# Cosine-similarity attention on one core: six shared PSUM banks for scores and transposes, and exponentials of three, two and three banks

## The chip, the core and the metric

The kernel runs on one core of one Trainium2 chip. The core has five engines that run side by side and meet only at semaphores: TensorE (PE in the profile, its weight loads PEld), VectorE (DVE), ScalarE (ACT), GpSimd (POOL) and SyncE (SP), which here only issues transfers. Inputs and output lie in HBM, the working data in SBUF, and what TensorE computes lands in PSUM, which has eight banks of 512 fp32 columns for each of 128 partitions. The metric is device time in microseconds (us), the median over runs. Before the change it is 190.81 us (three runs, 190.81 to 190.95).

## What is computed

Q, K and V are fp32 of shape (8, 12, 512, 64): 96 heads of 512 rows and 64 columns. Each row of Q and K is divided by its length, the scores of a head are the dot products divided by tau = 0.1, and softmax weights of them are applied to V:

```
Q_norm = Q / (np.linalg.norm(Q, axis=-1, keepdims=True) + 1e-10)
K_norm = K / (np.linalg.norm(K, axis=-1, keepdims=True) + 1e-10)
scores = np.einsum('bhqd,bhkd->bhqk', Q_norm, K_norm) / tau
weights = np.exp(scores - np.max(scores, axis=-1, keepdims=True))
weights = weights / (np.sum(weights, axis=-1, keepdims=True) + 1e-10)
return np.einsum('bhqk,bhkd->bhqd', weights, V).astype(np.float32)
```

A score lies between -10 and 10, so the kernel leaves the maximum out and takes exp(score / tau) as it is. The sum of the weights comes out of the product with V, through a column of ones beside V.

## The kernel before

The 96 heads are worked on as 48 pairs (index s, from 0 to 47). The work on a pair is a chain of small operations, each with a name:

- LD and LV: transfers of Q, K (into the tile qk) and V (vf), issued by SP.
- SQ: squares of Q and K, on POOL (on ACT for a part of the first three pairs).
- RED: the row sums of the squares, on DVE, one for Q (w = 0) and one for K (w = 1). For K, and for both in the first pairs, PE first adds eight slices into a corner of an output bank (SSQ), and DVE reduces what is left.
- NEW: one over the square root of the sums, for a group of 1, 2 or 4 pairs. Groups 1 to 3 (one pair each) do it on ACT (LOG, then NEW), the others in eight or nine short dependent steps on DVE.
- SCL: Q and K times that root, giving bf16 (qn). Q is scaled on DVE, K on POOL or, for ten pairs, on DVE.
- TR: eight transposes on PE into PSUM; EVA: one DVE copy of them into SBUF (qt).
- SCO: scores. A key chunk c (128 keys) of head h is one matmul with 64 rows of the array and 512 columns, so it fills one PSUM bank. Head 0 uses array rows 0 to 63 and head 1 rows 64 to 127.
- EXP: ACT reads score banks and writes exp of them in bf16 (et).
- PV: for each head four groups (t) of four small matmuls, et as weights and V with the column of ones as data, into an output bank (o_ps[h]).
- RCP and NRM: DVE takes the reciprocal of the sums and multiplies; ST: the transfer out. VC on POOL turns V into bf16.

The eight PSUM banks are dealt out so: four for scores (scps), two for outputs (ops), one for transposes (tps), one for the norm work (nps). The four score banks are used in two halves. One EXP takes 1024 columns, that is, chunk c of both heads; while ACT works on one half PE refills the other. So a pair is four SCOs of two matmuls and four EXPs. In pair 0 the first two chunks are taken head by head (four EXPs of 512 columns), and the last chunk of pair 47 is cut in three pieces (256, 512, 256 columns) so that the last products can start early.

The order of the work is written out by hand, one list of operation numbers for each engine (ORDER, L574). Each engine runs its list in order and waits for the operations that its next one needs (Program.run, L41). The lines that matter below: the scores are issued at L446 and the exponentials at L469 (the last pieces at L460), PV at L486 (L514 for the last pair), the transposes at L410 (L256 and L254 in pair 0), EVA at L417 (L267 in pair 0), SCL at L404, SSQ at L342, RED at L349 and L353, the root on ACT at L367 and L370 and on DVE at L377 to L386, NRM at L499 and L527, and the last stores at L531.

Of the kernel before, what the change touches and what calls it, by code (L numbers as in the profile page):

```python
# [8 lines left out]
class Op:  # L9
    def __init__(self, key, eng, kind, due, needs, emit, slot=None):  # L10
        self.key, self.eng, self.kind, self.due, self.emit = key, eng, kind, due, emit
        self.needs, self.slot = [n for n in needs if n is not None], slot
        self.own = False
        self.sem, self.val, self.inc, self.used = None, 0, 0, False
        self.start = self.end = None


class Program:


    def __init__(self, nc):
        self.nc, self.ops, self.list = nc, {}, []

    def add(self, key, eng, kind, due, needs, emit, **kw):
        assert key not in self.ops, key
        op = Op(key, eng, kind, due, needs, emit, **kw)
        self.ops[key] = op
        self.list.append(op)
        return op

    def schedule(self):
        order = {}
        for e, text in ORDER.items():
            order[e] = [self.list[int(x)] if x[0] != "-" else self.dummy(int(x[1:])) for x in text.split()]
        assert len(self.list) == len({o.key for v in order.values() for o in v if o.key != "dummy"})
        return order

    def dummy(self, columns):
        return Op("dummy", "pe", "", 0, [], lambda e: self.fill(e, columns))

    def run(self):  # L41
        nc = self.nc
        order = self.schedule()
        dma_sems, dma_count, last_out = {}, {}, {}
        for e, ops in order.items():
            for o in ops:
                o.waits = [self.ops[n] for n in o.needs]
                if e in ("pe", "act") and not o.own:
                    o.waits = [p for p in o.waits if p.eng != e]
                for p in o.waits:  # L50
                    p.used = True
        for e, ops in order.items():
            sem, count = nc.alloc_semaphore(f"s_{e}"), 0
            for o in ops:
# [8 lines left out]
                elif o.used:  # L63
                    count += 1
                    o.sem, o.val, o.inc = sem, count, 1

        def write(engine, name):
            seen = {}
            for o in order[name]:
                want = {}  # L70
                for p in o.waits:
                    k = id(p.sem)
                    if p.val > max(seen.get(k, 0), want.get(k, (None, 0))[1]):
                        want[k] = (p.sem, p.val)
                for k, (sem, val) in want.items():
                    engine.wait_ge(sem, val)
                    seen[k] = val
                inst = o.emit(engine)
                if o.sem is not None:
                    inst.then_inc(o.sem, o.inc)  # L80
# [26 lines left out]
def bass_cosine_similarity_attention_kernel(  # L107
# [11 lines left out]
    NP = BATCH * NHEAD // 2  # L119
    MAGIC = float(0x5F375A86)  # L120
# [13 lines left out]
    et = [sb(f"et{i}", [128, NT, 2, SEQ], bf16) for i in range(R_ET)]  # L134
    ob = [sb(f"ob{i}", [128, 2, NT, DIM], f32) for i in range(R_O)]
    rd = [sb(f"rd{i}", [128, 2, NT], f32) for i in range(R_O)]
    ys = [sb(f"ys{i}", [128, 64], f32) for i in range(R_X)]
    xs = {g: sb(f"xs{g}", [128, 64], f32) for g in NORM_ON_ACT}
# [6 lines left out]
    sc_ps = nc.alloc_psum_tensor("scps", [128, 4, SEQ], f32)  # L145
    o_ps = [nc.alloc_psum_tensor(f"ops{b}", [128, 512], f32) for b in range(2)]
    t_ps = nc.alloc_psum_tensor("tps", [128, 2, NT, 128], bf16)
    t_k0 = sc_ps[:, 3, :].bitcast(bf16)[:, 0:SEQ].rearrange("p (t x) -> p t x", t=NT)
    n_ps = nc.alloc_psum_tensor("nps", [128, R_X, 160], f32)
# [3 lines left out]
    sizes, left = [], NP  # L153
    for n in GROUPS:
        sizes.append(min(n, left))
        left -= sizes[-1]
        if not left:
            break
    while left:
        sizes.append(min(GROUPS[-1], left))  # L160
        left -= sizes[-1]
    group, first = [], []
    for g, n in enumerate(sizes):
        first.append(len(group))
        group += [g] * n
# [8 lines left out]
    P.add("one", "pool", "one", -100, [], lambda e: e.memset(ones[:, :], 1.0))  # L174
    P.add("eye", "pool", "sm_pool", -99, ["one"], lambda e: e.affine_select(  # L175
        out=ident[:, :], in_=ones[:, :], pattern=[[1, 128]], base=0, channel_multiplier=-1,
        compare_op=ALU.is_equal, fill=0.0))
    P.add("eps", "pool", "sm_pool", -98.5, [], lambda e: e.memset(eps[:, :], 1e-19))
    P.add("table", "act", "table", -900, [], lambda e: e.preload_act_table_set("natural_log_exp_and_others"))
    P.add("vone", "pool", "vone", -98, [], lambda e: e.memset(  # L180
# [7 lines left out]
    P.fill = lambda e, n: e.matmul(out=sc_ps[:, 0, 0:n], lhsT=ident[:, :], rhs=warm_in[:, 0:n], start=True, stop=True)  # L188
    P.add("wz", "dve", "sm_dve", -100, [], lambda e: e.memset(warm_in[:, :], 0.0))
    P.add("warm", "pe", "warm", -100, ["eye", "wz"], warm)  # L190

    def due_sq(s):
        g = group[s]
        return START + PERIOD * first[g] - 7.6 + (1.9 if g in NORM_ON_ACT else 0) - 3.43 * (first[g] + sizes[g] - 1 - s) - slack(s, M_SQ)

    def due_red(s):
        return due_sq(s) + 2.0

    slots = sorted((START + PERIOD * (s + 1) + 0.9 * PV_AT[4 * h + 3] + 0.05 + late(s), s, h) for s in range(NP - 1) for h in range(2))
    session, attached, early = {}, {}, []  # L200
    for s, w in sorted(((s, w) for s in range(NP) for w in range(2) if on_pe(s, w)), key=lambda j: (due_red(j[0]), j)):
        at = due_red(s) + 0.3
        if s < EARLY:
            early.append((s, w))
            continue
        due, i, h = next(x for x in slots if x[0] >= at and (x[1], x[2]) not in attached)
        attached[i, h] = (s, w)
        session[s, w] = (h, due, [("PV", i, h, NT - 1)])
    before = [[], []]
    for s, w in sorted(early):  # L210
        session[s, w] = (w, due_red(s), before[w])
        before[w] = [("RED", s, w)]
    bank_free = {}
    for s in range(NP):
        for h in range(2):
            bank_free[s, h] = before[h]
            before[h] = [("NRM", s, h)] + ([("RED",) + attached[s, h]] if (s, h) in attached else [])

    def head0(TF):
        for h in range(2):  # L220
            at = -100 + h
            x4 = [xs[0][:, 8 * w + 4 * h : 8 * w + 4 * h + 4] for w in range(2)]
            for w in range(2):
# [6 lines left out]
                P.add(("SQ", 0, w, h), SQ0[w][h], {"act": "sqah", "dve": "sqvh", "pool": "sqph"}[SQ0[w][h]], at + 0.1 * w,  # L230
                      [("LD", 0, w, h)] + (["table"] if SQ0[w][h] == "act" else []), emit)
                P.add(("RED", 0, w, h), "dve", "redh", at + 0.2 + 0.1 * w, [("SQ", 0, w, h)],
                      lambda e, w=w, x4=x4, dst=dst: e.tensor_reduce(out=x4[w], in_=dst, axis=AX.X, op=ALU.add))
            cols = lambda t, h=h: t[:, 0:16].rearrange("p (w x) -> p w x", w=2)[:, :, 4 * h : 4 * h + 4]
            P.add(("LOG", 0, h), "act", "ln", at + 0.4, [("RED", 0, 0, h), ("RED", 0, 1, h), "eps", "table"],
                  lambda e, cols=cols: e.activation(out=cols(ys[0]), in_=cols(xs[0]), func=ACT.Ln, bias=eps[:, :]))
            r_ps = sc_ps[:, 1, 0:4] if h == 0 else n_ps[:, 0, 128:132]
            for w in range(2):
                P.add(("NRMS", 0, w, h), "act", "sm_act", at + 0.5 + 0.01 * w, [("LOG", 0, h)],
                      lambda e, w=w, h=h, r_ps=r_ps: e.activation(  # L240
                          out=xs[0][:, 8 + 4 * h : 12 + 4 * h] if w else r_ps,
                          in_=ys[0][:, 8 * w + 4 * h : 8 * w + 4 * h + 4], func=ACT.Exp, scale=-0.5)).own = True
# [304 lines left out]
EARLY = 4  # L547
PE_BOTH = 4
K_ON_DVE = (1, 2, 3, 4, 9, 15, 21, 27, 33, 39)
VLAG = 3  # L550
# [143 lines left out]
```

## Time and profile before

| what | value |
|---|---|
| median of three runs | 190.81 us |
| span of the profiled execution, first to last instruction | 188.7 us |
| what lies around the span (the median less the span) | 2.1 us |
| ACT busy | 182.1 us (96%) |
| PE busy, ends modelled | 176.0 us (93%) |
| DVE busy | 164.9 us (87%) |
| POOL busy | 155.0 us (82%), all of it before about 165 us |
| DMA engines | 269 GB/s in the mean, most of it in the first 160 us |
| granted TensorE clock | full in all 40 slices of the span |

A row of the groups gives the source line, engine, operation, output and inputs with their shapes, how many instructions there are, how long the engine was busy with them in all, the mean length of one in ns, and what the engine waited for just before. The length of one instruction is longer than the distance to the next one: instructions of one engine overlap, and the distance is what counts for the sum. The chain of waits follows the work that ended last back to the start. In the timeline each line is a run of like instructions with its start, its length from first start to last end, and its count.

### The profile page before, as it was taken

The page shows a single profiled execution, that of the slowest core. Times are in us where ns is not written, and L with a number is a line of the kernel's source. Part 1 is how long each engine was busy: PE and PEld are TensorE (multiplying, and loading weights), DVE is VectorE, ACT ScalarE, POOL GpSimd, SP SyncE. Part 2 cuts the span into 40 slices and gives each one's busy share as a digit, 9 for nine tenths or more (in the row PEclk, how much of TensorE's full clock was granted, in tenths as well). Part 3 has the DMA queues.
Part 4 walks back from the last instruction along what each step waited for, and adds up shares of the span by engine and source line. Part 5 has one row for each costly group of instructions (what it writes and reads, how often), then busy time and mean ns, then how long its engine had stood idle before and what let it go on. Part 6 is the DMA issues. An engine that isn't in the chain of part 4 may idle for free.

```text
span 188.7 us, 6679 instructions
## 1 busy us (share of the span) xinstructions
PE 176.0 (93%) x2726; PEld 110.1 (58%) x2726; DVE 164.9 (87%) x530; ACT 182.1 (96%) x214; POOL 155.0 (82%) x145
## 2 busy tenths in 40 slices
PE   6998999999999999999999999999999999899992
PEld 2555666566665666566666566665666556555552
DVE  2789999999999899999999989998889987977543
ACT  4899999999999999999999999999999999999992
POOL 5689999999999999999999899999699898260000
PEclk9999999999999999999999999999999999999999
DMA  4999999999999978999898997997999943113133
GB/s 153 345 352 351 349 357 322 311 315 377 381 385 354 296 264 261 349 335 299 270 255 256 378 344 233 300 314 223 280 326 336 326 139 113 59 56 115 56 114 111
DMA packets 52445, 50.75 MB, mean 269 GB/s; under 512 B 3136, under 2 KB 52416, under 8 KB 52416
## 3 DMA queue, kind: packets, MB, share of 16 engines
q1 hardware_dynamic: 51984, 50.02, 81.6%
q8 instruction: 21, 0.34, 0.7%
q10 hardware_dynamic: 432, 0.33, 0.5%
q14 instruction: 8, 0.07, 0.1%
HBM read 37.75 MB, written 12.58 MB: 267 GB/s over the span
## 4 chain that ended last, share of the span: by engine, by line
ACT 94%; DMA 3%; SPq 1%; issue 1%; DVE 1%; PE 0%
ACT et L469 92%; DMA qk<-in_Q_dram 3%; SPq L299 0%; SPq L296 0%; ACT et L460 0%; DVE ob L527 0%; ACT sq L317 0%; ACT ys L367 0%; ACT nps L370 0%; PE ops L514 0%; DVE rd L525 0%
## 5 line engine op out<-in xcount | busy, mean ns | idle before, releaser
L469 ACT ACTIVATE et<-scps 128x1024 bf16<-128x1024 f32 (+1 forms) x193 | 175.8, 1247 | 0.0
L325 POOL TENSOR_TENSOR sq<-qk 128x1024 bf16<-128x1024 f32 x44 | 82.7, 1891 | 2.0 <-DMA qk<-in_K_dram 2.0
L446 PE MATMUL scps<-qt 64*128 64x512 bf16 x384 | 75.5, 385 | 7.4 <-ACT et L469 2.3
L486 PE MATMUL ops<-vb,et 128*128 128x65 bf16 x1504 | 74.5, 194 | 0.0
L486 PEld LDWEIGHTS ops<-vb,et 128*128 128x128 bf16 x1504 | 56.1, 98 | 27.9 <-issue 21.5
L404 POOL TENSOR_TENSOR qn<-qk,rk 128x512 bf16<-128x512 f32 x37 | 38.1, 1041 | 6.4 <-DVE rk L382 6.1
L499 DVE TENSOR_TENSOR ob<-ops,rd 128x256 f32<-128x256 f32 x94 | 39.3, 420 | 0.9
L404 DVE TENSOR_TENSOR qn<-qk,nps 128x512 bf16<-128x512 f32 x57 | 38.1, 678 | 0.4 <-ACT nps L370 0.4
L417 DVE COPY qt<-tps 128x1024 bf16<-128x1024 bf16 x47 | 32.3, 688 | 4.1 <-PE tps L410 3.4
L446 PEld LDWEIGHTS scps<-qt 64*128 64x128 bf16 x384 | 19.4, 92 | 26.1 <-ACT et L469 10.1
L410 PE MATMUL tps<-ident,qn 128*128 128x128 bf16 x376 | 33.0, 221 | 0.1
L474 POOL TENSOR_SCALAR vb<-vf 128x512 bf16<-128x512 f32 x48 | 29.3, 624 | 0.7 <-PE tps L410 0.7
L353 DVE TENSOR_REDUCE nps<-sq 128x8 f32<-128x512 bf16 x44 | 29.7, 683 | 0.0
L410 PEld LDWEIGHTS tps<-ident,qn 128*128 128x128 bf16 x376 | 21.4, 98 | 12.0 <-issue 5.7
L497 DVE RECIPROCAL rd<-ops 128x4 f32<-128x4 f32 x94 | 16.6, 177 | 9.2 <-PE ops L486 5.8
L342 PE MATMUL ops<-sq,ident 128*128 128x64 bf16 x400 | 20.0, 193 | 0.0
L342 PEld LDWEIGHTS ops<-sq,ident 128*128 128x128 bf16 x400 | 14.9, 98 | 4.1 <-issue 2.9
L349 DVE TENSOR_REDUCE nps<-ops 128x8 f32<-128x64 f32 x44 | 9.3, 211 | 0.8 <-PE ops L342 0.7
L377 DVE TENSOR_TENSOR nps<-nps,ys 128x32 f32<-128x32 f32 (+1 forms) x30 | 6.3, 208 | 0.2
L378 DVE SCALAR_TENSOR_TENSOR nps<-nps,ys 128x32 f32<-128x32 f32 (+1 forms) x30 | 6.2, 207 | 0.2
L185 PE MATMUL ops<-warm_in,ident 128*128 128x512 bf16 x8 | 3.6, 631 | 1.4 <-POOL ident L175 1.4
L319 POOL TENSOR_TENSOR sq<-qk 128x512 bf16<-128x512 f32 (+1 forms) x4 | 3.7, 933 | 1.2 <-DMA qk<-in_K_dram 1.0
(50 smaller groups left out, 40.8 us busy)
## 6 DMA issues: line engine op xcount, KB each, us to landing
vf<-in_V_dram SPq DMA_DIRECT2D x48, 256.0 KB, 5.3
qk<-in_Q_dram SPq DMA_DIRECT2D x47, 256.0 KB, 4.3
qk<-in_K_dram SPq DMA_DIRECT2D x47, 256.0 KB, 5.4
out_dram<-ob SPq DMA_DIRECT2D x47, 256.0 KB, 3.5
qk<-in_Q_dram SPq DMA_DIRECT2D x2, 128.0 KB, 2.7
qk<-in_K_dram ACTq DMA_DIRECT2D x2, 128.0 KB, 2.9
out_dram<-ob SPq DMA_DIRECT2D x1, 128.0 KB, 1.7
out_dram<-ob ACTq DMA_DIRECT2D x1, 64.0 KB, 1.6
```

The costliest lines, as they stand in the source:

```text
L325: lambda e: e.tensor_tensor(out=sqf, in0=data, in1=data, op=ALU.mult))
L342: last = e.matmul(out=o_ps[bank][:, 320:384], lhsT=ident[:, :], rhs=sq[iqs][:, 8 * w : 8 * w + 8, 8 * k : 8 * k + 8], start=(k == 0), stop ...
L353: lambda e, w=w, dst=dst: e.tensor_reduce(out=dst, in_=sq[iqs][:, 8 * w : 8 * w + 8, :], axis=AX.X, op=ALU.add))
L404: lambda e, w=w, r=r: e.tensor_tensor(out=qn[iqn][:, w].rearrange("p t h d -> p h t d"), in0=qk[iq][:, w].rearrange("p h (t d) -> p h t d" ...
L410: last = e.transpose(t_ps[:, w, t, :], qn[iqn][:, w, t].rearrange("p h d -> p (h d)"), ident[:, :])
L417: lambda e: e.tensor_copy(out=qt[iqt][:, :, :, :].rearrange("p w t x -> p (w t x)"), in_=t_ps[:, :, :, :].rearrange("p w t x -> p (w t x)")))
L446: last = e.matmul(out=sc_ps[:, 2 * b + h, :], lhsT=qt[iqt][64 * h : 64 * h + 64, 1, c, :], rhs=qt[iqt][64 * h : 64 * h + 64, 0, :, :], sta ...
L469: lambda e, c=c, b=b, hs=hs: e.activation(out=et[iet][:, c, hs[0] : hs[-1] + 1, :], in_=sc_ps[:, 2 * b + hs[0] : 2 * b + hs[-1] + 1, :], f ...
L474: lambda e: e.tensor_scalar(out=vb[:, iq, :, :, 0:DIM].rearrange("p c h d -> p h c d"), in0=vf[iv][:, :, :].rearrange("p h (c d) -> p h c ...
L486: last = e.matmul(out=o_ps[h][:, 65 * t : 65 * t + 65], lhsT=et[iet][:, c, h, 128 * t : 128 * t + 128], rhs=vb[:, iq, c, h, :], start=(c = ...
L497: lambda e, h=h, grid=grid: e.reciprocal(out=rd[io][:, h, :], in_=grid[:, :, DIM]))
L499: lambda e, h=h, grid=grid: e.tensor_tensor(out=ob[io][:, h], in0=grid[:, :, 0:DIM], in1=rd[io][:, h, :].unsqueeze(2).to_broadcast([128, N ...
```

## The change

- PSUM is dealt out anew: six banks form one ring that scores and transposes share, and two banks take outputs (numbers 6 and 7, o_ps[0] and o_ps[1]). The transpose bank and the norm bank are gone.
- From pair 9 on (WIDE = 9) the eight score banks of a pair go to ACT as three EXPs of 3, 2 and 3 banks in place of four of 2. The ring is used in halves of three: pair s takes banks 0-2, 3-4, 0-2 or 3-5, 0-1, 3-5 by turns. The third bank of the half that has only two banks of scores takes the transposes of the next pair. Pairs 1 to 8 keep four EXPs of two banks (banks 0-1 and 3-4), with transposes in bank 2.
- In pair 0 and pair 47 the scores go head by head (by_head): pair 0 in EXPs of 1, 1, 2, 2, 2 banks, pair 47 in 3, 2, and then 1280 and 256 columns. The spare bank for the last piece of the last product is the first bank of the middle half of the ring, where it was the transpose bank.
- Norm work: the sums (xs) and the running product (ys) lie in SBUF. The running root and the result lie in output bank 6, in columns 384 and up, and for groups 2 to 6 in ring bank 5. The DVE scaling reads its factor from there. All SSQ go to a corner of bank 7. In groups where K of some pair is scaled on DVE the result for Q and K is one step in place of two.
- Orders: one sequence over all engines in place of five lists. From it the program takes each engine's order, and it adds a wait between any two operations of different engines that touch the same bank, in the order of the sequence (link). Waits that earlier waits imply are left out. The ring of scaled tiles (qn) has four buffers in place of three. The orders of all engines are new; in pair 0 the LOG of group 1 stands after the second EXP and its NEW after the third, where they stood after the first.

The core of the diff:

```diff
-RINGS = 18, 10, 6, 3, 3, 3, 8, 3
+RINGS = 18, 10, 6, 4, 3, 3, 8, 3
+FIRST, FIRST_BANKS = (1, 1, 2, 2, 2), (0, 1, 3, 0, 3)
+WIDE = 9
+TURN0 = (2, 5)
+ROOT_BANK = {2: 5, 3: 5, 4: 5, 5:5, 6:5}
...
-    sc_ps = nc.alloc_psum_tensor("scps", [128, 4, SEQ], f32)
+    ring = nc.alloc_psum_tensor("ring", [128, 6, SEQ], f32)
     o_ps = [nc.alloc_psum_tensor(f"ops{b}", [128, 512], f32) for b in range(2)]
-    t_ps = nc.alloc_psum_tensor("tps", [128, 2, NT, 128], bf16)
-    n_ps = nc.alloc_psum_tensor("nps", [128, R_X, 160], f32)
+    O = (6, 7)
...
+    def by_head(s):
+        return s in (0, LAST)
+
+    def unit(s, c, h):
+        return NT * h + c if by_head(s) else 2 * c + h
+
+    plan, turn_bank, uses = [], {}, []
+    for s in range(NP):
+        lo, hi = (0, 3) if s < WIDE or (s - WIDE) % 2 == 0 else (3, 0)
+        turn_bank[s] = lo + 2
+        if s < WIDE:
+            counts = FIRST if s == 0 else (2, 2, 2, 2)
+            banks = FIRST_BANKS if s == 0 else (0, 3, 0, 3)
+        else:
+            counts, banks = (3, 2, 3), (lo, hi, lo)
...
+    def link(self, sequence):
+        touched = {}
+        for n, o in enumerate(sequence):
+            o.place = n
+            o.waits = [self.ops[k] for k in o.needs]
+            for b in o.banks:
+                last = touched.setdefault(b, {})
+                o.waits += [p for e, p in last.items() if e != o.eng and p not in o.waits]
+                last[o.eng] = o
...
+            def sco(e, units=units, b=b):
+                for k, (c, h) in enumerate(units):
+                    last = e.matmul(
+                        out=ring[:, b + k, :], lhsT=qt[iqt][64 * h : 64 * h + 64, 1, c, :],
+                        rhs=qt[iqt][64 * h : 64 * h + 64, 0, :, :], start=True, stop=True)
+                return last
...
+            for k, (lo, hi) in enumerate(((0, 1280), (1280, 1536)) if (s, j) == (LAST, 2) else ((0, n * SEQ),)):
+                P.add(("EXP", s, j + k), "act", f"exp{hi - lo}", [("SCO", s, j), "table"] + values,
...
+        xg, tg = xs[g % R_X][:, 0 : 2 * m], ys[g % R_X][:, 0 : 2 * m]
+        yg = bank[:, ROOTS : ROOTS + 2 * m]
+        rg = bank[:, col : col + 2 * m]
...
-                        t_ps[:, w, t, :], qn[iqn][:, w, t].rearrange("p h d -> p (h d)"), ident[:, :])
+                        turned(turn_bank[s])[:, w, t, :], qn[iqn][:, w, t].rearrange("p h d -> p (h d)"), ident[:, :])
```

Three stretches of the new sequence, its numbers turned into the names above (key chunk and head left out where they do not matter; w after a dash):

```
pair 1's start    ACT: SQ-2 EXP-0-0 EXP-0-1 LOG-1 EXP-0-2 NEW-1 EXP-0-3 EXP-0-4 LOG-2 NEW-2 EXP-1-0
                  PE:  SCO-0-0 SCO-0-1 SCO-0-2 SSQ-1-1 TR-0 SSQ-2-0 SCO-0-3 SSQ-2-1 SCO-0-4 TR-1-1
                       PV-0(1) SSQ-3-0 TR-1-0 PV-0(5) SSQ-3-1 SCO-1-0
                  DVE: RED-2-0 SCL-1-1 SCL-1-0 RED-2-1 RED-3-0 EVA-1 SCL-2-0
pair 22           EXP-22-0 | SCO-22-1 TR-23-1 TR-23-0 PV-21(4) EXP-22-1 | SCO-22-2 SSQ-29-1 EXP-22-2
pair 47's end     PE:  ... EXP-47-2 then PV-47 of both heads, the last after EXP-47-3
                  DVE: RCP-47-0 RCP-47-1 RCP-47-2 NRM-47-1 NRM-47-2 NRM-47-0
                  SP:  ST-47-0 ST-47-2
```

## The prediction

> **What bounds the kernel now.** I read the page's busy shares and chain first, then the chain in order of time, then ACT's groups by shape, then the timeline of PE, ACT and DVE at the start and in the middle.
>
> ```profile
> PE 176.0 (93%) x2726; PEld 110.1 (58%) x2726; DVE 164.9 (87%) x530; ACT 182.1 (96%) x214; POOL 155.0 (82%) x145
> ACT 94%; DMA 3%; SPq 1%; issue 1%; DVE 1%; PE 0%
> ...
> 14.79 169.56 ACT et L469 x185
> 184.34 0.78 ACT et L460 x2
> ```
>
> The chain is one row of exponentials: 185 of them in 169.56 us, 0.9165 us each, with nothing between. The kernel is ACT's time plus a start of some 8 us and an end of 3.3 us (last EXP's end, 185.39, to 188.73).
>
> ```profile
> L469 ACT ACTIVATE et<-scps 128x1024 bf16<-128x1024 f32 x189 | 173.6, 1261 | 0.0
> L469 ACT ACTIVATE et<-scps 128x512 bf16<-128x512 f32 x4 | 2.1, 586 | 0.0
> L317 ACT ACTIVATE sq<-qk 128x512 bf16<-128x512 f32 x2 | 1.3, 630 | 0.4 <-DMA qk<-in_Q_dram 0.3
> L317 ACT ACTIVATE sq<-qk 128x256 bf16<-128x256 f32 x1 | 0.4, 417 | 0.1
> ```
>
> From 256 to 512 columns a square grows by 213 ns, 0.832 ns a column. So 1024 columns are 852 to 853 ns of 916.5, and what one EXP costs beside its columns is 63 ns. As a check, the last two pieces (512 and 256 columns) take 0.77 us of the chain: 0.64 for columns, 64 each.
>
> ```profile
> 8.96 0.60 PE L446 MATMUL scps<-qt 64*128 64x512 bf16 x2
> 101.03 0.39 PE L446 MATMUL scps<-qt 64*128 64x512 bf16 x2
> 10.64 1.03 ACT L469 ACTIVATE et<-scps 128x1024 bf16<-128x1024 f32 x1
>   ACT et L469: 12.3, 57
> ```
>
> Two scores on different halves of the array take 0.39 us together; the two of 8.96, both of head 1, take 0.60, so a second one on the same half comes 0.22 later. An EXP that starts on an idle engine takes 1.03 us against 0.917 of the row: scores must be there 0.113 before the EXP ahead ends. The last line (the scores' own idle times) says that PE stood waiting for ACT before a weight load or a score 57 times for 192 score pairs; at the others it was already late, within what the buffers forgive.
>
> **The change, part by part.** All against the profiled execution's span of 188.73; 2.1 us lie around it to the median, which I take as unchanged.
>
> Fewer EXPs. Pairs 9 to 46 drop one each: 38 x 63 ns = 2.41 us. Pair 0 drops one of six and pair 47 two of six: 0.06 and 0.13. Gain 2.60. The longest piece in the trace has 1024 columns; a 1536-column one is bounded by 1.28 (columns alone) and 1.83 (two rows of 0.917). I take 1.343, since 256, 512 and 1024 lie on one line.
>
> The Trainium skill, "ScalarE: Activation LUTs", on what ACT_TABLE_LOAD costs, gives 186 ns beside the columns with an overlap of about 93 ns, so at least 93 per EXP. By it the gain would be an estimated 3.8 us; the row has 63, and the sum goes by the row.
>
> Scores of three banks. Two run side by side, the third comes 0.22 later: ready 0.60 after the first, 0.22 more PE time, twice per pair. Against this goes one switch from full-array work to half-array work, which costs about 0.10 + 0.10 around each score pair (0.32 from the score at 101.03 to the next product at 101.35, of which about 0.22 is the matmul). So PE work per pair stays near 3.3 us of a pair time that falls from 3.667 to 3.603, and PE does not become the bound. The tight place is SCO-s-2: released by EXP-s-0, due before EXP-s-1 (0.917) ends. Release 0.06 (0.05 to 0.11 in the trace), three matmuls 0.60, to ACT 0.04, 0.113 ahead: 0.81. Margin 0.11, where the old pair had 0.32. In the sequence I added what PE does between SCO-s-1 and SCO-s-2: at most 1.34 us (pairs 17 and 22), and PE may take 1.45. So it fits, with 0.1 to spare; I charge 0.2 us in all for small misses (bounds 0 and 38 x 0.11 = 4.2, if PE is a full margin late beyond it in every pair).
>
> The Trainium skill, "TensorE: Matmul & The Clock Gate", Part 3 on packing small matmuls, says that a weight load overlaps a running matmul only when the row group differs. That speaks against this change: the third score's load (92 ns in the trace) would come on top, 0.69 instead of 0.60, and the margin would be 0.02. The trace's 0.60 already holds a same-half pair with its load, so the load is hidden there.
>
> Transposes in the ring. TR of pair s+1 may start only when EXP-(s-1)-2 has freed the bank, and EVA must be done before SCO-(s+1)-0. TR 0.6, EVA 0.69, against 0.917 + 1.343 until the scores may start: 0.9 to spare. Nothing, except where DVE is late. EVA-6 stands behind EXP-5-3 and a root step: 0.1 + 0.69 + 0.05 + 0.39 + 0.04 = 1.27 to the next EXP against 0.917, so ACT waits 0.35 there (bounds 0, if DVE runs ahead of the sequence, and 0.7). It is late because RED-10-0 before it on DVE needs SQ-10, which POOL, full from 10 us on, has done at about 30.
>
> Norm work in bank 6. DVE reads and writes there (RCP and NRM 0.6, SCL 0.68, roots 0.4 per pair, together 1.7 of 3.6 us), and products of head 0 (0.7) must keep out: waits added, no work. The products' place is after SCO-s-1; DVE's distances (0.6 for a reduction, a scaling, a copy, 0.33 for NRM, 0.1 for small steps) sum to 3.1 us in a mean wide pair, so it is on time: 0 (bounds 0 and 2.4, see the rivals). Fewer root steps in seven groups take 0.1 to 0.2 us each off DVE, hidden. Sums into SBUF cost DVE 0.01 each, hidden. Redundant waits left out: 0 to -0.1.
>
> The start. Loads, squares and the first EXP at 8.08 stay: that EXP waits for the transfer that ends at 7.52. Then NEW-1 moves back.
>
> ```profile
> 9.20 0.68 DVE L404 TENSOR_TENSOR qn<-qk,nps 128x512 bf16<-128x512 f32 x1
> 10.08 0.68 DVE L404 TENSOR_TENSOR qn<-qk,nps 128x512 bf16<-128x512 f32 x1
> 11.25 0.69 DVE L417 COPY qt<-tps 128x1024 bf16<-128x1024 bf16 x1 [0.49 <-PE tps L410]
> 11.65 1.95 ACT L469 ACTIVATE et<-scps 128x1024 bf16<-128x1024 f32 x2
> ```
>
> Before, NEW-1 is done at 9.08, EVA-1 starts at 11.25 and pair 1's first EXP at 12.55 (the second of the last line), without a wait. After: EXP-0-0 8.08, EXP-0-1 8.56, LOG 9.14 (its sum waits for SSQ-1-1 behind four lone scores on PE), EXP-0-2 9.34, NEW-1 10.24 to 10.44; SCL-1-1 10.55, SCL-1-0 11.15 to 11.83; one product group, SSQ-3-0, TR-1-0 on PE to 12.63; EVA-1 12.68 to 13.37; SCO-1-0 ready 13.8; EXP-1-0 13.85. ACT was free at 12.6. Loss against before 1.25 (bounds 0.3, if products and SSQ do not delay TR-1-0 and DVE moves up, and 1.6).
>
> The end. SCO-47-2 is three scores of one head, ready 0.83 after its start, 0.13 late. After the last EXP before: reciprocal and multiply of the last piece, ST-47-2 issued 1.18 us after it.
>
> ```profile
> 186.16 0.82 SPq L531 DMA_DIRECT2D out_dram<-ob  x2
> 186.25 0.29 DVE L527 TENSOR_TENSOR ob<-tps,rd 128x128 f32<-128x128 f32 x1
> ```
>
> After: DVE does three reciprocals, then the multiplies of 0.29, 0.29 and, last, 0.42: NRM-47-0 ends about 1.45 after the last EXP. ST-47-0 waits for it, and ST-47-2, ready earlier, is queued behind it on SP 0.40 later: 1.87 in place of 1.18, 0.69 lost (bounds 0.2 and 1.0). Other loads and stores keep their number; POOL's and DMA's load is the same.
>
> Sum: -2.60 + 0.20 + 0.35 + 1.25 + 0.13 + 0.69 = +0.02. Span 188.75; with 2.1 around it 190.85, say 190.9: no change. Nothing under 0.2% (0.38 us) can be told from none.
>
> **The rivals.**
>
> First, late scores of three banks: SCO-s-2 misses its place. It decides once PE comes more than 0.11 late in the mean of 38 pairs; at 0.16 late ACT stands 0.05 each time, 1.9 us: 192.8, slower. For it: PE was late at two scores in three before; against it: the sequence leaves PE waiting there in most pairs.
>
> Second, the start and the end cost little: EXP-1-0 late by 0.3, EVA-6 not late, the stores 0.2 later. 0.95 + 0.35 + 0.49 = 1.8 less: 189.1; with half of it 190.0. For it: the sequence need not hold where an engine comes earlier; against it: each step of the reckoning is a row of the trace.
>
> Third, bank 6 becomes a wait: twelve root chains (groups from pair 10 on) of seven dependent steps of 0.23 keep products out for 1.6 us; where scores stand behind these products on PE, 0.2 each, 2.4 us: 193.3.
>
> Fourth, the wide EXP brings nothing: if a third bank costs as much as a new instruction, the 2.4 us fall away: 193.3.
>
> **How the numbers follow.** The reckoned sum 0.45 (own range 190.2 to 191.6: start, end and misses within half their bounds; a quarter of it faster, a quarter slower). Late scores 0.25. Cheap start and end 0.17. Bank 6 0.09, no gain per EXP 0.04. Faster: 0.11 + 0.17 = 0.28. Same: 0.22. Slower: 0.12 + 0.25 + 0.09 + 0.04 = 0.50. The range from 189.4 to 193.2 leaves out the cheapest start (under 0.05) and the dearest of the last cases (some 0.13).
>
> **What would show it.** EXPs of 1536 columns 1.34 us apart and ACT without idle time from pair 9 on carry the gain; idle time before EXPs released by scores, once per pair, is the first rival. EXP-1-0 near 13.85 and a gap near 32 us show the start; the last store issued 1.9 us after the last EXP shows the end. Wrong would be: idle ACT in the middle by DVE, or a first EXP that does not start at 8.1.

## The result, and the profile after

The changed kernel takes 202.0 us (median of four runs, 201.3 to 203.8) beside 190.8 for the kernel before on the same chip: 1.058 times as long, 95% interval 1.053 to 1.064. The forecast was 190.9, with a range to 193.2. The profiled execution has a span of 199.73 us, 11.0 more than before.

First the page of the changed kernel: busy time, the chain by engine, and the exponentials by shape (groups with shapes kept apart; the columns are count, busy us, mean ns, idle before and its releaser).

```profile
PE 179.6 (90%) x2729; PEld 108.2 (54%) x2729; DVE 163.2 (82%) x523; ACT 181.8 (91%) x173; POOL 155.0 (78%) x145
ACT 28%; DVE 27%; PE 22%; DMA 9%; POOL 9%; SPq 2%; issue 2%; DVEq 0%; POOLq 0%
...
L510 ACT ACTIVATE et<-ring 128x1536 bf16<-128x1536 f32 x77 | 109.4, 1488 | 6.2 <-PE ring L499 6.0
L510 ACT ACTIVATE et<-ring 128x1024 bf16<-128x1024 f32 x74 | 74.3, 1064 | 4.4 <-PE ring L499 4.3
```

Before, the chain was one row of exponentials, 94% ACT. Now ACT has 28% of it, and exponentials stood idle for scores. The chain in order of time, and what each engine waited for:

```profile
86.29 0.56 SPq L365
86.89 6.43 DMA qk<-in_K_dram
93.40 3.74 POOL sq L393 x2
97.14 1.01 POOL qn L473
98.20 0.61 PE ring L480 x4
99.03 0.96 PE ring L499 x2
...
120.83 5.99 DMA qk<-in_K_dram
126.89 1.89 POOL sq L393
128.78 1.00 POOL qn L473
...
139.24 6.24 DMA qk<-in_K_dram
145.55 1.89 POOL sq L393
147.44 1.01 POOL qn L473
...
153.42 38.50 ACT et L510 x32
```

```profile
POOL sq L393 <- DMA qk<-in_K_dram: 10.4, 8, 2.3
ACT et L510 <- PE ring L499: 10.3, 7, 2.9
...
POOL vb L516 <- DMA vf<-in_V_dram: 6.1, 4, 2.5
```

Three times the chain begins in the same way. A K transfer (pairs 31, 39 and 44), issued late by SP, lands. POOL has been waiting for it to square a pair that ACT needs only much later: from pair 24 on, 27 to 37 us after the square starts, the stalls included (23 to 30 before). Behind the square in POOL's order stands the K scaling of a pair that ACT needs within 5 us (SCL-24-1, SCL-32-1, SCL-36-1). PE waits for that scaling before a transpose (2.37, 2.15 and 2.47 us in its timeline), and scores behind the transpose come late. The first and the third time the chain itself goes on to PE. The second time it stays on POOL and shows a loop: from a late square at 134.42 it goes to sums and a multiply on DVE, to the store that waits for them (SP, 138.13), and to the K load of pair 44 behind that store, issued at 139.24, for which POOL waits again. Before, POOL waited 2.0 us for K at the same line of its code, and not for V:

```profile
POOL sq L325 <- DMA qk<-in_K_dram: 2.0, 5, 0.7
```

The whole difference can be laid out from the trace. Count for every exponential the distance of its end from the end of the one before, less 0.833 ns a column and 63.5 ns; what is left is lost time. The second row is thus reckoned with the price of an exponential (in brackets their number) and cannot confirm it; the price is measured below.

| us | before | after |
|---|---|---|
| first exponential starts | 8.08 | 8.07 |
| exponentials, by columns and 63.5 ns each | 176.34 (196) | 173.75 (155) |
| lost between them | 0.97 | 13.97 |
| last exponential's end to the span's end | 3.34 | 3.94 |
| span | 188.73 | 199.73 |

Of the 13.97 lost, 2.49 lie in the start, 0.55 at pair 6, 0.24 at pairs 7 and 9, 3.48 near 100 us (pairs 23 and 24), 2.09 near 131 (pair 31), 4.33 near 150 (pairs 35 and 36), 0.22 at the last pair, and the rest in pieces of under 0.2.

Why the K transfers came late is in the rows of SP and of the DMA engines, the latter in 40 slices of 5 us.

```profile
SPq L537 <- DVE ob L545: 57.8, 24, 6.0
```

The same row of the kernel before:

```profile
SPq L503 <- DVE ob L499: 48.0, 26, 3.5
```

Transfers of the changed kernel:

```profile
GB/s 177 348 352 347 349 357 380 382 329 351 380 363 263 197 356 304 248 304 297 340 111 249 308 205 303 350 175 319 276 281 43 271 153 191 75 96 64 60 101 105
```

SP issues stores and loads in one list, and stood 57.8 us at stores that wait for DVE. From 60 to 70 us the transfers fall from 350 to 380 GB/s to 263 and 197, though the loads behind the waiting store needed nothing but an issue: the buffer for pair 31 was free from 53.3 us on, and its K was issued at 86.9. None of this is new. SP stood 48.0 us before, and the transfers fell to 296, 264 and 261 GB/s from 61 to 75 us. What is new is when POOL wants the data: K of pair 31 landed at 93.06 before and at 93.33 now, and its square started at 99.37 before, while now POOL stood waiting for it 2.15 us.

### The profile page after: what moved, and what is told of

The parts are those of the page before. It is cut to its first block, busy times and chain, and to the rows that moved or that the text cites. A ratio compares the mean times of both kernels' runs of the same rounds, so it can differ in the third digit from the quotient of the medians.

```text
span 199.7 us, 6641 instructions
## 1 busy us (share of the span) xinstructions
PE 179.6 (90%) x2729; PEld 108.2 (54%) x2729; DVE 163.2 (82%) x523; ACT 181.8 (91%) x173; POOL 155.0 (78%) x145
## 2 busy tenths in 40 slices
DMA packets 52444, 50.75 MB, mean 254 GB/s; under 512 B 3136, under 2 KB 52416, under 8 KB 52416
## 4 chain that ended last, share of the span: by engine, by line
ACT 28%; DVE 27%; PE 22%; DMA 9%; POOL 9%; SPq 2%; issue 2%; DVEq 0%; POOLq 0%
ACT et L510 28%; DMA qk<-in_K_dram 9%; PE ring L499 7%; DVE qn L473 7%; PE ops L527 6%; POOL sq L393 6%; DVE ob L545 5%; DVE xs L420 4%; DVE qt L486 4%; PE ring L480 3%; POOL qn L473 2%; DVE rd L543 2%; PE ops L229 2%; PE ops L406 2%; DVE xs L414 2%
## 5 line engine op out<-in xcount | busy, mean ns | idle before, releaser
L510 ACT ACTIVATE et<-ring 128x1536 bf16<-128x1536 f32 (+3 forms) x155 | 176.1, 1265 | 10.8 <-PE ring L499 10.3
L499 PE MATMUL ring<-qt 64*128 64x512 bf16 x384 | 78.1, 389 | 2.8 <-ACT et L510 1.9
L480 PE MATMUL ring<-ident,qn 128*128 128x128 bf16 x376 | 34.6, 223 | 10.8 <-POOL qn L473 7.0
L545 DVE TENSOR_TENSOR ob<-ops,rd 128x256 f32<-128x256 f32 (+1 forms) x96 | 40.0, 419 | 0.5
L486 DVE COPY qt<-ring 128x1024 bf16<-128x1024 bf16 x47 | 32.2, 686 | 9.3 <-PE ring L480 9.1
L480 PEld LDWEIGHTS ring<-ident,qn 128*128 128x128 bf16 x376 | 21.9, 99 | 22.4 <-POOL qn L473 8.7
L420 DVE TENSOR_REDUCE xs<-sq 128x8 f32<-128x512 bf16 x44 | 29.5, 677 | 1.6 <-POOL sq L393 1.5
L473 DVE TENSOR_TENSOR qn<-qk,ops 128x512 bf16<-128x512 f32 x45 | 29.2, 673 | 0.7 <-ACT ops L434 0.6
L543 DVE RECIPROCAL rd<-ops 128x4 f32<-128x4 f32 x96 | 16.9, 178 | 14.9 <-PE ops L527 13.3
L499 PEld LDWEIGHTS ring<-qt 64*128 64x128 bf16 x384 | 16.1, 93 | 16.4 <-ACT et L510 5.8
L406 PE MATMUL ops<-sq,ident 128*128 128x64 bf16 x400 | 20.3, 195 | 0.6 <-DVE xs L414 0.3
L406 PEld LDWEIGHTS ops<-sq,ident 128*128 128x128 bf16 x400 | 15.1, 99 | 9.6 <-issue 3.3
L414 DVE TENSOR_REDUCE xs<-ops 128x8 f32<-128x64 f32 x50 | 10.3, 207 | 1.6 <-PE ops L406 1.4
```

The lines of the kernel that those rows point to most:

```text
L406: last = e.matmul(out=o_ps[1][:, SUMS : SUMS + 64], lhsT=ident[:, :], rhs=sq[iqs][:, 8 * w : 8 * w + 8, 8 * k : 8 * k + 8], start=(k == 0) ...
L420: lambda e, w=w, dst=dst: e.tensor_reduce(out=dst, in_=sq[iqs][:, 8 * w : 8 * w + 8, :], axis=AX.X, op=ALU.add))
L473: lambda e, w=w, r=r: e.tensor_tensor(out=qn[iqn][:, w].rearrange("p t h d -> p h t d"), in0=qk[iq][:, w].rearrange("p h (t d) -> p h t d" ...
L480: last = e.transpose(turned(turn_bank[s])[:, w, t, :], qn[iqn][:, w, t].rearrange("p h d -> p (h d)"), ident[:, :])
L486: lambda e: e.tensor_copy(out=qt[iqt][:, :, :, :].rearrange("p w t x -> p (w t x)"), in_=turned(turn_bank[s]).rearrange("p w t x -> p (w t ...
L499: last = e.matmul(out=ring[:, b + k, :], lhsT=qt[iqt][64 * h : 64 * h + 64, 1, c, :], rhs=qt[iqt][64 * h : 64 * h + 64, 0, :, :], start=Tr ...
```

## The experiments

In the diffs the lists of operation numbers are written with the operations' names, and for one engine. Theory A: POOL, squaring far ahead, meets K and V that have not landed. Rival B: the shared banks and scores of three banks leave no slack. Rival C: a lower TensorE clock makes PE late. Four kernels went first.

**Loads earlier (e1_loads).**

```diff
 SP, around pair 31; the same for pairs 19 to 47
-ST-16 LV-25 LD-29-0 LD-29-1 ST-17 LV-26 LD-30-0 LD-30-1 ST-18 LV-27 LD-31-0 LD-31-1 ST-19
+ST-16 LV-25 LD-31-0 LD-31-1 ST-17 LV-26 LD-32-0 LD-32-1 ST-18 LV-27 LD-33-0 LD-33-1 ST-19
```

As the diff shows, a load passes two stores (ST-18 and ST-17 for pair 31); the text below counts one too few, and so does that of e5_loads2.

> The changed kernel with the Q and K loads of pairs 19 to 47 moved one store earlier in SP's order; nothing else. Theory A (POOL runs its squares 28 to 37 us ahead of use, meets K loads that have not landed, and urgent K scalings stand behind it): the three stalls near 100, 131 and 150 us (9.9 us together) are gone, POOL's wait for K loads falls from 10.4 us to under 4, and the time is about 192.1 us (191.4 to 194). Rival B (the shared banks and scores of three banks leave no slack, whatever POOL does): the stalls stay, 200 to 203 us. Rival C (a lower TensorE clock makes PE late): the clock still dips and the time is above 198 us.

Measured 193.3 and 194.5 us, ratio 1.016 (1.011 to 1.021). A third run took 197.3. The execution that was profiled took 788.8 us, with all matmuls several times as long; it says nothing of the edit and is left out. Moving loads alone takes back some 8 of the 11 us, so B and C as sole causes fall; the next run has the usable profile.

**The four squares behind the scalings (e2_pool).**

```diff
 POOL
-... SQ-31 SQ-30 SCL-24-1 SCL-25-1 SCL-26-1 ...
+... SCL-24-1 SCL-25-1 SQ-31 SCL-26-1 SQ-30 ...
-... SQ-39 SCL-32-1 ...
+... SCL-32-1 SQ-39 ...
-... SQ-44 SCL-36-1 SCL-37-1 ...
+... SCL-36-1 SCL-37-1 SQ-44 ...
```

> The changed kernel with four squares moved on POOL alone: SQ-31 behind SCL-25-1, SQ-30 behind SCL-26-1, SQ-39 behind SCL-32-1, SQ-44 behind SCL-37-1; all loads stay as late as they are. Theory A: what hurts is the scalings behind the waiting squares, so the stalls at pairs 24, 32 and 36 go (2.9 to 3.5, 1.9 to 2.1 and about 4.3 us), the squares themselves still wait for K loads, and the time is 192 to 196 us. Rival D (the transfers themselves are late, so that the squares' sums and the roots come late too, and the stall only moves): 198 us or more. Rival B: 200 to 203 us.

Measured 200.6 us, ratio 1.051 (1.047 to 1.056): my own form of theory A missed, rival D held. Rival B's range holds this time as well; e1_loads and e5_loads2 tell the two apart. SCL-24-1 came 1.6 us earlier (95.5), but the stall went on to pair 24 (3.58 and 0.52 us lost near 105 us) and from pair 31 to pairs 33 and 34 (2.29 and 0.85). The chain of this kernel shows why:

```profile
95.53 2.05 POOL qn L473 x2
97.57 1.85 POOL sq L393
99.43 1.00 POOL qn L473
100.43 1.86 POOL sq L393
102.29 0.04 issue
102.33 0.61 PE ops L406 x8
```

L406 is the sum of the square on PE (SSQ-30-1). It too stands early in PE's order, and scores stand behind it. With late inputs, moving one victim makes the next one: squares, sums and roots all run early, in every engine's list.

**Back to exponentials of two banks (e3_narrow).**

```diff
-WIDE = 9
+WIDE = 47
 and in the order, for pairs 9 to 46
-SCO-s-0(3 banks) SCO-s-1(2) SCO-s-2(3)
+SCO-s-0 SCO-s-1 SCO-s-2 SCO-s-3 (2 each), the third halfway to the fourth
```

> The kernel of the earlier loads, with pairs 9 to 46 back on four exponentials of two banks (banks 0, 3, 0, 3, all transposes in bank 2); everything else in its order. Theory A with the price of the prediction (63 ns for each exponential beside its columns): 38 more exponentials, 2.4 us above the kernel with earlier loads, some 194.5 us (193.8 to 196.5). Rival E (the wide exponential brings nothing): the same time as the kernel with earlier loads, within 0.5 us. Rival B (scores of three banks cost ACT idle time that scores of two do not): at or below the kernel with earlier loads.

Measured 200.8 us, ratio 1.050 (1.045 to 1.056), 6 to 8 more than e1_loads, on which it stands, where 2.4 was expected. The profile has 9.95 us lost in some thirty pieces (the largest 1.63 and 1.00), and its POOL waited 10.1 us for V. An order made for pieces of three, two and three banks does not fit four of two; the run says only that going back does not help. It does not give the price of an exponential, which e9_split measures.

**Later loads in the kernel before (e4_before_late).**

```diff
 SP of the kernel before, pairs 20 to 47
-ST-19 LV-28 LD-31-0 LD-31-1 ST-20 LV-29 LD-32-0 LD-32-1 ST-21 LV-30 LD-33-0 LD-33-1
+ST-19 LD-29-0 LD-29-1 LV-28 ST-20 LD-30-0 LD-30-1 LV-29 ST-21 LD-31-0 LD-31-1 LV-30
```

> The kernel before, with the Q and K loads of pairs 20 to 47 moved two stores later in SP's order (some 7 us); nothing else. Theory A: K lands up to 7 us later against squares that had 0.1 to 6.3 us to spare, POOL waits for K loads and its scalings come late; their lead to the pair's first exponential is 4 to 15 us, so ACT stands idle at some pairs: 194 to 201 us. Rival B (the layout of the changed kernel is what makes it sensitive): 190.5 to 191.5 us, as before.

Measured 232.7 us, ratio 1.218 (1.213 to 1.223). The direction is theory A's; the size is 42 us, where I expected 3 to 10.

```profile
POOL sq L325 <- DMA qk<-in_K_dram: 40.5, 17, 6.1
ACT et L469 <- PE scps L446: 36.6, 29, 5.0
DVE nps L353 <- POOL sq L325: 29.4, 12, 6.2
```

POOL's 40.5 us of waiting for K come back almost whole as 36.6 us of ACT waiting for scores. The old layout is sensitive too, so the sensitivity is not the new layout's alone. The loop of the changed kernel's chain (load, square, sum, store, next load) fits the size; here it was not followed link by link.

**Loads three stores earlier, V two (e5_loads2).**

```diff
 SP, around pair 31; the same for pairs 19 to 47 (V: 18 to 47)
-ST-15 LV-24 LD-28-0 LD-28-1 ST-16 LV-25 LD-29-0 LD-29-1 ST-17 LV-26 LD-30-0 LD-30-1 ST-18 LV-27 LD-31-0 LD-31-1
+ST-15 LD-31-0 LD-31-1 LV-26 ST-16 LD-32-0 LD-32-1 LV-27 ST-17 LD-33-0 LD-33-1 LV-28 ST-18 LD-34-0 LD-34-1 LV-29
```

> The changed kernel with the Q and K loads of pairs 19 to 47 two stores earlier in SP's order and the V loads of pairs 18 to 47 one store earlier; nothing else. Theory A (late inputs for POOL's early squares and copies): POOL waits under 3 us for K and under 3 us for V; what is left against the kernel before is the start, the sixth pair and the end, 188.7 - 2.6 + 1.5 + 0.5 + 0.3 + 0.2 + 0.6 = 189.2 of span, 191.3 us (190.8 to 192.5). Rival D (the transfers cannot come earlier, since the queues are full until some 75 us): no better than with one store, 193 to 195 us, with stalls left in the middle. Rival B: 198 us or more.

Measured 192.5 us, ratio 1.008 (1.005 to 1.011): 9.5 us less than the changed kernel, by transfers issued in another order and nothing else. Its waits of POOL, exponentials and transfers:

```profile
POOL sq L393 <- DMA qk<-in_K_dram: 0.4, 2, 0.3
...
POOL vb L516 <- DMA vf<-in_V_dram: 0.2, 1, 0.2
```

```profile
L510 ACT ACTIVATE et<-ring 128x1536 bf16<-128x1536 f32 x77 | 109.4, 1494 | 0.0
L510 ACT ACTIVATE et<-ring 128x1024 bf16<-128x1024 f32 x74 | 74.6, 1067 | 1.8 <-PE ring L499 1.6
```

```profile
GB/s 154 339 350 347 348 347 380 378 379 382 377 384 377 380 349 377 299 264 300 309 297 310 246 264 273 351 319 267 328 194 114 207 116 59 55 113 55 97 71 110
```

K of pair 31 is issued at 76.6 in place of 86.9 us, POOL no longer waits, the three stalls are gone, and the dip in slices 13 and 14 is filled (377 and 380). The row shows no idle time before a 1536-column exponential in the whole kernel. SP stood at stores about as long as the kernel before (49.8 us), but the loads now stand ahead of these stores. Theory A is shown; B falls, since layout and work are untouched. The time is at the upper end of the range. How much of it is V's and not K's was not taken apart, and no run put all squares back to their old places, so that this would help as much is not shown.

The clock is no cause of its own, since it stayed full once the loads alone were moved, but it seems to enlarge a stall. Windows of the changed kernel around the first one (stretch and its length, busy us of PE, its weight loads, DVE, ACT and POOL with instruction counts, then granted clock, DMA share, GB/s), then the first two windows of e5_loads2:

```profile
93.00:97.00 4.00, 2.67 (x36) 1.28 (x33) 3.58 (x13) 4.00 (x4) 3.60 (x2) 1.00 0.98 322
97.00:101.00 4.00, 2.80 (x29) 1.78 (x30) 1.28 (x2) 1.21 (x2) 4.00 (x6) 0.64 0.98 327
101.00:105.00 4.00, 4.00 (x70) 2.50 (x71) 3.02 (x8) 3.63 (x4) 4.00 (x6) 0.93 0.18 61
```

```profile
93.00:97.00 4.00, 3.64 (x61) 2.19 (x58) 3.96 (x14) 4.00 (x5) 4.00 (x4) 1.00 0.99 342
97.00:101.00 4.00, 4.00 (x67) 2.38 (x63) 4.00 (x11) 4.00 (x4) 4.00 (x7) 1.00 0.92 294
```

In the changed kernel the clock falls to a mean of 0.64 in the window in which PE ends a stand of 2.37 us, and three scores then take 1.03 us in place of 0.60 (timeline of PE, changed kernel, then e5_loads2):

```profile
98.20 0.61 PE L480 MATMUL ring<-ident,qn 128*128 128x128 bf16 x4 [2.37 <-POOL qn L473]
...
98.96 1.03 PE L499 MATMUL ring<-qt 64*128 64x512 bf16 x3
```

```profile
98.18 0.60 PE L499 MATMUL ring<-qt 64*128 64x512 bf16 x3
```

The three stalls differ in this. The clock was 0.50 from 98.1 to 101.5 and from 149.3 to 152.7 us, at the end of stands of 2.37 and 2.47 us, and ACT lost 3.48 and 4.33 us. Near 130 us PE stood 2.15 us, the clock stayed full, and ACT lost 2.09. That the slow clock makes up all of the 1.1 and 1.9 us by which the two cost more than PE stood is argued from three cases, not shown.

**The price of an exponential (e9_split).** On the kernel of e5_loads2:

```diff
-e.activation(out=et[... lo : hi], in_=ring[... lo : hi], func=ACT.Exp, scale=inv_tau)
+[e.activation(out=et[... x : y], in_=ring[... x : y], func=ACT.Exp, scale=inv_tau)
+ for x, y in ([(lo, 1024), (1024, hi)] if hi - lo == 3 * SEQ else [(lo, hi)])][-1]
```

> The kernel of e5_loads2 with each exponential of 1536 columns issued as two instructions, 1024 and 512 columns, in the same banks: 77 more instructions, all else the same. By the prediction's price (63 ns each): 4.9 us more than e5_loads2, 197.4 us (196.8 to 198.2). If a third bank costs as much as an instruction of its own (rival E): the same time as e5_loads2 within 0.5 us. By 93 ns each, the lower bound worked out in the prediction from the Trainium skill's page, it would be an estimated 7.2 us.

Measured 197.0 us, ratio 1.031 (1.028 to 1.034), 4.55 above the median of e5_loads2 (forecast 4.9). Between the medians of two kernels that is 59 ns each. The traces give the price without a sum. From the end of one exponential to the end of the next, in the medians from 50 to 180 us, 1536 columns take 1.343 us in e5_loads2; 1024 take 0.917 and 512 take 0.490 in e9_split. The two pieces take 1.407, so the extra instruction costs 63 to 64 ns, and from 1024 to 1536 columns the distance grows by 0.833 ns a column. Rival E falls.

The Trainium skill, "ScalarE: Activation LUTs", on what ACT_TABLE_LOAD costs, gives 186 ns less an overlap of 93, so at least 93 each; by it 77 would be an estimated 7.2 us. The run disagrees with the page and the measurement decides. The profiled execution had a mean granted clock of 0.944 (e5's 0.995) and lost about 0.5 us more between its exponentials. The three other runs had 0.994 to 1.000 and took 196.6 to 197.4 us, it 197.8; why its clock was lower is not known.

**Start, pair 6 and end.** These try the other terms of the prediction, and look for a version that beats both kernels. All stand on e5_loads2.

```diff
 e6_start: the chain of pair 1 earlier
-SCO-0-2 EXP-0-0 EXP-0-1 SSQ-1-1 RED-1-1 LOG-1 EXP-0-2 NEW-1
+SSQ-1-1 RED-1-1 SCO-0-2 EXP-0-0 EXP-0-1 LOG-1 NEW-1 EXP-0-2
-PV-0-1-1 PV-0-1-2 SSQ-3-1 SCO-1-0 SCO-1-1
+SCO-1-0 SCO-1-1 PV-0-1-1 PV-0-1-2 SSQ-3-1
```

> The kernel of e5_loads2 with pair 1's chain moved up: the sum SSQ-1-1 ahead of the third score of pair 0, LOG-1 and NEW-1 ahead of the third exponential, and two products and SSQ-3-1 behind the first two scores of pair 1. By the prediction's own term for the start (1.25, measured 1.5) 1.0 to 1.3 us less than e5_loads2, first exponential of pair 1 near 12.9 us in place of 14.0. If something else holds that exponential (the copy EVA-1, the banks), it stays at 13.5 or later and the time falls by under 0.5 us.

Measured 192.6 us (1.007, 1.005 to 1.010): no gain. The first exponential of pair 1 lost 1.13 instead of 1.63 us, but LOG-1 and NEW-1 in a row cost 0.33 more, and pair 6 lost 1.00 in place of 0.63.

```diff
 e7_all: e6_start and
-VC-5 SCL-6-1      -RCP-3-0 NEW-6-0 NRM-3-0 TR-6-1 EVA-6
+SCL-6-1 VC-5      +TR-6-1 EVA-6 RCP-3-0 NEW-6-0 NRM-3-0
 the end: PV, RCP and NRM of head 0 of pairs 46 and 47 first; last stores
-NRM-47-1 NRM-47-2 ST-47-1 NRM-47-0 ST-47-0 ST-47-2
+NRM-47-0 ST-47-0 NRM-47-1 ST-47-1 NRM-47-2 ST-47-2
```

> The kernel of e6_start, and two more orders: the K scaling of pair 6 ahead of a V copy on POOL and its copy EVA-6 ahead of small work on DVE; at the end head 0 of the last two pairs first, so that the last store of the longer piece does not stand ahead of the last one. By the prediction's terms (0.35, measured 0.55, and 0.69, measured 0.60) 0.8 to 1.1 us less than e6_start: 188.8 to 189.8 us, faster than the kernel before by 0.5 to 1.0%. If the end is set by the last transfer alone, the last part brings nothing and it is 189.6 to 190.4.

Measured 192.4 us (1.006, 1.004 to 1.009). The end did what was expected: from the last exponential to the span's end 3.27 us instead of 3.96. But pairs 5 and 6 lost 2.2 us in place of 0.6.

e11_end has that end alone (and one product of pair 46 behind the last scores):

> The kernel of e5_loads2 with the end alone put in another order: head 0 of the last two pairs first, the last store that of the last piece. By the prediction's term for the end (0.69; 0.60 measured in the changed kernel) the time from the last exponential's end to the end of the span falls from 4.0 to 3.3 us and the whole by 0.6 to 0.7: 191.8 us (191.4 to 192.2). If another transfer ends as late, under 0.2.

Measured 191.9 us (1.004, 1.002 to 1.006), 0.62 less than e5_loads2, with 3.27 from the last exponential to the end. The prediction's term was 0.69. The two kernels ran on different chips (the kernel before at 191.15 and 191.03), and their intervals just overlap, so the trace's 0.69 is the better evidence. Its profiled execution took 192.6: the clock was 0.50 from 12.4 to 15.8 us, and the first exponential of pair 1 lost 2.99 us where e5_loads2, with the same order there, lost 1.63.

Three more orders of the first 45 us; e8_best and e10_best2 also have the end of e7_all:

```diff
 e8_best: start as in e6 with TR-1-0 right behind TR-1-1; around pair 6
-SQ-10 VC-5 SCL-6-1 SQ-11 SCL-7-1     RED-8-1 RED-8-0 SSQ-9-1 NEW-5-6 NEW-5-7
+SCL-6-1 SCL-7-1 VC-5 SQ-10 SQ-11     NEW-5-6 NEW-5-7 RED-8-1 RED-8-0 SSQ-9-1
 e10_best2: e8_best and
-PV-4-0-0 ... PV-4-0-3 SCO-6-0 SCO-6-1 PV-5-0-0 TR-7-0 ... TR-7-1 ... EVA-7
+SCO-6-0 SCO-6-1 TR-7-0 TR-7-1 PV-4-0-0 ... PV-4-0-3 EVA-7 PV-5-0-0
 e12_best3: e11_end, the start of e8, and around pair 6
+SCO-5-1 TR-6-0 TR-6-1 SSQ-9-1 EVA-6 ... SCL-6-1 SQ-10 SCL-7-1 VC-5 ... SCO-6-0 PV-4-0-0 ... SCO-6-1
```

> The kernel of e5_loads2 with four orders redone after e6 and e7: (1) in the start, besides e6's moves, both transposes of pair 1 ahead of products, and three products behind the first scores of pair 1; (2) around pair 6 the root of group 5 ahead of pair 8's sums, the K scalings of pairs 6 and 7 ahead of SQ-10 on POOL, and pair 10's and 11's sums later; (3) the end of e7_all; (4) one product behind the last scores. Theory: e7 failed at pair 6 because the scaling still stood behind SQ-10 on POOL, and at the start because three products stood between the transposes and the scores. Start 1.1 to 1.4 us less than e5_loads2, pair 6 0.5 to 0.6 less, end 0.6 to 0.7 less: 192.5 - 2.4 = 190.1 us (189.6 to 190.8), first exponential of pair 1 within 0.3 us of the end of what stands before it on ACT. If POOL's squares are bound by the loads in this stage, pair 6 or 8 is late all the same and it is 190.8 to 191.8.

> The kernel of e8_best with four more moves: the first scores of pair 6 ahead of the four products that wait for NRM-3-0, the transposes and the copy EVA-7 of pair 7 right behind them, SSQ-11-1 behind the first scores of pair 7, SSQ-4-1 behind the last scores of pair 1 (in e8 TensorE stood 1.15 us at the products, 0.60 at SSQ-11-1 and 0.74 at SSQ-4-1). Theory: ACT's idle time at pair 6 (1.17), pair 7 (0.77 + 0.24) and pair 8 (0.47) falls to 0.4 in all, and 0.3 goes in pairs 2 and 3: about 2.5 us less than e8_best, 191.0 us; against e5_loads2 1.5 less. If POOL's and DVE's squares and sums are the bound of this stage, the idle time comes back at pair 8 or 10 and the time stays above 192.

> The kernel of e11_end (earlier loads, new end) with the start of e8_best and one more order around pairs 5 to 7: both transposes and the copy EVA-6 of pair 6 right behind the second scores of pair 5, the K scaling of pair 6 ahead of SQ-10 on POOL, that of pair 7 behind it, the scores of pair 6 ahead of or between the products that wait for DVE. Theory: the start's 0.8 is then not lost again at pair 6 to 8, as it was in e6, e8 and e10, and 0.5 of pair 6's own goes too: 191.9 - 1.1 = 190.8 us (190.2 to 191.4), the kernel before or just under it. If the stage up to pair 8 is bound by POOL's squares and DVE's sums whatever their order (e6, e8 and e10 would be three signs of it), it is 191.7 to 193.5.

Measured 193.6 (1.015, 1.011 to 1.019), 194.2 (1.018, 1.014 to 1.022) and 192.8 us (1.010, 1.008 to 1.012). The start itself was mended: from the first exponential to that of pair 1 it is 4.85 us in e8, against 5.92 in the changed kernel and 4.47 before. But the time went again within 30 us: e8 lost 1.17 at pair 6 and 0.77 at pair 7, e10 lost 1.52 within pair 6, e12 lost 0.36 to 0.49 in each of five places from pair 5 to pair 7. From 10 to 147 us POOL is busy 90% or more in every slice of e5_loads2, and in e8 PE waited 0.74 us at 16.9 us for a square that had waited 0.28 us for its load. That the stage is bound by POOL's squares and DVE's sums fits these misses; it is argued, not shown, and against it stands that POOL was nearly as full before, where nothing was lost from pair 2 to pair 8. No version beat the kernel before; the best is e11_end, 0.4% slower than it.

## Why the prediction was wrong, step by step

The step that failed is the last line of "The end": "Other loads and stores keep their number; POOL's and DMA's load is the same." It was costed at nothing. The loads did stay the same (POOL 155.0 us busy in both, 50.75 MB), but I asked how much work there was and not in what order each list meets it. In SP's list the Q and K loads stand only one store earlier than before (from pair 17 on), while POOL's squares moved further: SQ-31, for one, stood ahead of SCL-28-1 in POOL's list and now stands ahead of SCL-24-1. In e5_loads2, which has the same order on POOL and no such stalls, the squares of pairs 24 to 47 start 4.3 us further ahead of their pairs than before in the median, and those of pairs 31, 39 and 44, at which the stalls began, 9.5, 4.6 and 8.0. The trace of before had shown that K landed only 0.1 to 6.3 us before POOL used it from pair 12 on. Moving the loads took back 9.5 us (e5_loads2). None of the four rivals was this one either.

| step | predicted | measured |
|---|---|---|
| 41 fewer exponentials of 63 ns | -2.60 | 63 to 64 ns each by the distances of e9_split, which makes -2.6 |
| 1536 columns | 1.343 | 1.343; and 1.203 in the mean of 3, 2 and 3 banks without a wait, where (2 x 1.343 + 0.917) / 3 is 1.201 |
| misses of three-bank scores | +0.20 | about 0.5 in e5_loads2, in four pieces of 0.09 to 0.18 |
| EVA-6 | +0.35 | 0.55 |
| start | +1.25 | 1.52; first exponential of pair 1 at 13.99, forecast 13.85 |
| SCO-47-2 | +0.13 | 0.22 |
| end | +0.69 | 0.60; e11_end won back 0.69 in the trace, 0.62 in the median |
| loads, POOL's order | 0 | 9.5 |

- The rate of the wide stretch was right: after 153.42 us the chain has 32 exponentials in 38.50 us, 1.203 each. "Late scores" (first rival) and "the wide EXP brings nothing" (fourth) fall by that row and by e5_loads2.
- The row "ACT et L510 <- PE ring L499: 10.3, 7" looks like the first rival's sign, idle time released by scores. But it counts seven waits and not one per pair, and the chain leads from them to a scaling, a square and a load.
- The weight load of the third score is hidden, as the row of before had it: three scores take 0.60 us in e5_loads2 (98.18). The Trainium skill, "TensorE: Matmul & The Clock Gate", Part 3, where a load overlaps only a matmul of another row group, would have had 0.69 as an estimate; this trace does not show it.
- "Bank 6 becomes a wait" (third) is not seen in the middle of e5_loads2: nothing above 0.19 is lost from pair 9 to pair 46.
- "Start and end cost little" (second) is wrong for the start. Some 0.65 of what is left between the profiles of e5_loads2 and of the kernel before is a first exponential that started at 8.73 instead of 8.08; it scatters from run to run.
- With loads on time the change is still no gain: the 2.6 us saved are given back by the start, pair 6, small misses and the end, much as the sum had said (+0.02, against +0.9 in the profiles without the late first exponential).

## What to carry to other kernels

When a change rewrites an order, compare for each queue how far it runs ahead, not only how much it has to do: here the distance from a load's issue to its first reader and from there to the engine that sets the pace. Loads that share an in-order queue with stores wait for the end of the pipeline, and a reader moved ahead of them turns that into a stall. To find out, move the loads alone.

## What the runs showed of the hardware that was not expected

- The granted TensorE clock was halved (0.50) for 3.4 us at a time, twice in the changed kernel: from 98.1 us, after TensorE had stood 2.37 us for one wait, and from 149.3, after 2.47. After a stand of 2.15 us it stayed full. At 0.50 three scores took 1.03 us instead of 0.60, and the two stalls cost ACT more than TensorE had stood (3.48 and 4.33 us), the third did not (2.09).
- Two stores' delay of the loads in the kernel before cost 42 us, not the 3 to 10 expected; in the changed kernel's chain a late square delays a store, and that store the next load.
- The first exponential started between 8.07 and 9.54 us in eleven profiles of kernels whose first loads are the same. The old start was profiled twice, in the kernel before (8.08) and in e4_before_late (7.96), so how much it scatters there is open.
- One execution took 788.8 us at a shown clock of 1.000, with six warm-up matmuls taking 3.95 us that take 1.13 otherwise. Why is not known.
